# Loading the memory of a cross-attention in four transfers, one feature in eight to a partition

## The chip, the cores and the metric

One core of a Trainium2 chip runs the whole kernel. Its engines work side by side and meet at semaphores: TensorE (PE in the profile; PEld is its weight load), VectorE (DVE), ScalarE (ACT), GpSimd (POOL) and SyncE (SP), which here only starts transfers. ACT and POOL start some transfers too. The metric is the device time of one execution in microseconds; lower is better. Where several executions were timed, the median is used.

## The reference

Two layers of a hybrid network over 256 tokens of 1024 features, batch 1, all in float32. Each layer has four sublayers with a layer norm behind each:

```
for l in range(2):
    h = layer_norm(ALPHA * h + 0.5 * swiglu(h, ffn1_gate[l], ffn1_up[l], ffn1_down[l]))
    z = h @ w_in[l]                      # conv, recurrence and pool from slices of z
    h = layer_norm(ALPHA * h + mix @ w_out[l])
    h = layer_norm(ALPHA * h + cross_attn(h, mem, ca_q[l], ca_k[l], ca_v[l], ca_o[l]))
    h = layer_norm(ALPHA * h + 0.5 * swiglu(h, ffn2_gate[l], ffn2_up[l], ffn2_down[l]))

def cross_attn(x, mem, wq, wk, wv, wo):
    q, k, v = x @ wq, mem @ wk, mem @ wv          # 4 heads of 256
    return softmax(q k^T / 16) v @ wo
```

`mem` is 256 rows of 1024 features. It is an input, the same for both layers, and enters only as `mem @ ca_k[l]` and `mem @ ca_v[l]`: sums over the 1024 features, whose order may be chosen as long as memory and weights use the same one. The feed-forward width is 2816.

## The kernel before

Every float32 product is made of three passes on PE: each operand is split into a rounded part (`hi`, written by ACT as a cast) and the rest (`lo`, written by DVE as a difference), and hi·hi, hi·lo and lo·hi are summed in PSUM. `split` (L74 to L76) makes both parts, so "L75 ACT" and "L76 DVE" in the profile are the parts of weights (`whi`, `wlo`) and of activations. All matmuls are issued from `product` (L126).

Weights come through `load` (L78): DMAs on SP's queue into `raw` buffers (six of 128x1024), then splits into `whi` and `wlo` (eight each). A buffer is used again as soon as its last reader is through, so SP's transfers, the casts on ACT and the differences on DVE each wait for those that released the buffer. Each queue works strictly in its own order. That order comes from a scheduler with its own estimates of time, except in stretches under `manual_schedule`.

A feed-forward net (`ffn`, L420) runs over its 2816 hidden columns in chunks of 512. Chunks 2 and 4 go by `by_seven` (L594), a scheme that needs seven half-products in the place of eight: it adds blocks of weights to each other before multiplying. The blocks are `w00`, `w01`, `w10`, `w11`. Three sums are made on DVE (L624), and two in the transfer itself: `more(w01, up, 1)` and `more(w00, gate, 1)` load a further block on POOL's queue with `accum_op=add` onto what lies there (L658, two transfers of 512 KB each). The second pair can start once DVE has split the earlier contents of `w00`. Its order on PE: `run(o[0], ..., w00)`, `run(o[1], bx[0], ...)`, `run(o[2], ...)`, a slab of the down projection, `run(o[0], bx[1], ...)`, another slab, `run(o[0], bx[2], ...)`, `run(o[3], bx[3], ...)`, `run(o[0], part_of_x(1, 1), parts_of(w00), True)`. Twice between these, `taken` (L653) lets ACT copy the running sum out of `o[0]` before PE adds to it again: `taken(e, o[0])` ahead of the run with `bx[2]`, and `taken(f, o[0])` ahead of the last run, which uses the `w00` of the accumulating transfer. `w00` of chunk 4 lies in the buffers `lng` and `lnb`, into which SP later loads the layer norm's parameters (L316, L317).

The memory is fetched once, during the first feed-forward net. In `load_memory` (L204), called at chunk 3 (L766), 32 transfers on POOL's queue (L213) put feature kP+p into partition p: for each of 8 groups of 128 features and 4 quarters of 32 partitions, 256 runs of 128 bytes (32 features of one row). A small copy ahead of them (L765) holds them until chunk 2's activations exist. They land as 32x32 blocks lying side by side, still turned the wrong way. At chunk 5, `later` (L218) has DVE transpose each block (L222, four instructions of 128x512, reading adjacent elements) and split the result into `mT`. Between L222 and the layer norm behind the net (`finish`, L323), DVE has the last splits of weights, the sums L352 and the norm itself (L362 to L378); PE then transposes the normed rows (L193), first of the first 128 tokens.

`keys` (L789) and `values` (L799) load `ca_k` and `ca_v` by `load` and multiply them with `mT`.

Of the kernel before, what the change touches and what calls it, by code (L numbers as in the profile page):

```python
# [17 lines left out]
P = 128  # L18
DEPTH = 2
SEQ = 256  # L20
DM = 1024
DFF = 2816
NT = SEQ // P
NK = DM // P
# [4 lines left out]
CHUNK = 512  # L29
# [31 lines left out]
def model(ctx: ExitStack, tc: tile.TileContext, t: dict, out: bass.AP):  # L61
    nc = tc.nc
# [5 lines left out]
    def acc(shape=(P, 2, SEQ), tag="acc"):  # L68
        return ps.tile(list(shape), F32, tag=tag, name=tag)


    loads, normed, lows = [], [], []

    def split(hi, lo, src):  # L74
        nc.scalar.copy(hi, src)  # L75
        lows.append(nc.vector.tensor_tensor(lo, src, hi.bitcast(F32), op=ALU.subtract))  # L76

    def load(src, k0, nk, c0, ncol, fine=False, dealt=False):  # L78


        hi, lo, todo = [], [], []
        step = 2048 // ncol
        for a in range(k0, k0 + nk, step):
            half = step // 2
            raw = [
                wp.tile([P, 1024], F32, tag="raw", name="raw", bufs=6).rearrange("p (k c) -> p k c", c=ncol)
                for _ in range(2)
            ]
            part = 1 if fine else half
            for b in range(0, step, part):  # L90
                to = raw[b // half][:, b % half : b % half + part, :]
                if dealt:

                    c, u = divmod(a // 2, 2)
                    at = slice(c * CHUNK + 2 * P * b, c * CHUNK + 2 * P * (b + 1))
                    rows = src[at, c0 : c0 + ncol].rearrange("(p u) c -> p u c", u=2)[:, u, :]
                    loads.append(nc.sync.dma_start(to[:, 0, :], rows))
                else:
                    loads.append(nc.sync.dma_start(
                        to, src[(a + b) * P : (a + b + part) * P, c0 : c0 + ncol].rearrange("(k p) c -> p k c", p=P)  # L100
                    ))
            for s in range(2):
                h = wp.tile([P, 1024], F32R, tag="whi", name="whi", bufs=8)
                w = wp.tile([P, 1024], F32R, tag="wlo", name="wlo", bufs=8)
                h = h.rearrange("p (k c) -> p k c", c=ncol)
                w = w.rearrange("p (k c) -> p k c", c=ncol)
                r = raw[s]
                if fine:
                    todo += [(h[:, b, :], w[:, b, :], r[:, b, :]) for b in range(half)]
                else:  # L110
                    split(h, w, r)
                hi.append(h)
                lo.append(w)
        return Weights(hi, lo, half, todo)
# [3 lines left out]
    def halves(a):  # L118
        return a.rearrange(
            "p (h c) -> p h c" if len(a.shape) == 2 else "p r (h c) -> p r h c", h=2  # L120
        )
# [7 lines left out]
    def sums(o):  # L129
        return o.rearrange("p (c h) -> p h c" if len(o.shape) == 2 else "p r (c h) -> p r h c", h=2)  # L130
# [4 lines left out]
    def mm_cols(w, cols, x):  # L135
        o = acc()
        for k in range(NK - 1):
            product(o, w.at(k, cols)[0], x[:, k], k == 0, False)
        for k in range(NK):
            product(o[:, 0, :], w.at(k, cols)[1], x[:, k, 0, :], False, False)  # L140
        product(o, w.at(NK - 1, cols)[0], x[:, NK - 1], False, True)
        return sums(o)

    def add(dst, o):
        dst = dst if len(dst.shape) == 3 else halves(dst)
        nc.scalar.copy(dst, o[:, 1])
        nc.vector.tensor_tensor(dst, o[:, 0], dst, op=ALU.add)


    def mm_rows(o, xh, xl, wh, wl, start, stop, more=False):  # L150
        product(o, xh, wh, start, False, more)
        product(o, xh, wl, False, False, more)
        product(o, xl, wh, False, stop, more)

    def tok(i):
        return slice(i * P, (i + 1) * P)
# [29 lines left out]
    early_rows, early_memory = (cst.tile([P, 2048], F32, tag=f"mT{n}", name=f"early{n}") for n in range(2))  # L186
# [15 lines left out]


    def load_memory(mp, behind):  # L204
        m = [
            early_memory[:, n * DM : (n + 1) * DM].rearrange("p (k b j) -> p k b j", k=4, j=32) for n in range(2)
        ]
        with tc.issue_after(behind.ins):
            for n in range(2):
                for a in range(4):  # L210
                    for k in range(4):
                        c = (4 * n + k) * P + a * 32
                        nc.gpsimd.dma_start(  # L213
                            m[n][a * 32 : a * 32 + 32, k],
                            t["mem"][0, :, c : c + 32].rearrange("(b i) j -> i b j", i=32),
                        )

        def later():  # L218
            for n in range(2):
                turned = mp.tile([P, NT, CHUNK], F32, tag="up", name="turned", bufs=1)  # L220
                for k in range(2):
                    nc.vector.transpose(turned[:, k, :], m[n][:, 2 * k : 2 * k + 2].rearrange("p k b j -> p (k b j)"))  # L222
                mT.tiles[n] = cst.tile([P, 4, 2, SEQ], F32R, tag=f"mT{n}", name=f"mT{n}")
                for k in range(2):
                    d = slice(4 * n + 2 * k, 4 * n + 2 * k + 2)
                    split(mT[:, d, 0, :], mT[:, d, 1, :], turned[:, k, :].rearrange("p (k t) -> p k t", k=2))

        return later
# [191 lines left out]
    def ffn(l, name, n, pend=None, last=False, early=None):  # L420
        gate, up, down = (t[f"{name}_{x}"][l] for x in ("gate", "up", "down"))
        with tc.tile_pool(name="ffn", bufs=2, reuse_waits="tile") as fp:
# [56 lines left out]
            def first():  # L479

                s = activations()
                wg = load(gate, 0, NK, 0, CHUNK, fine=pend is None)
                wu = load(up, 0, NK, 0, CHUNK) if pend is not None else None

                if pend is None:
# [8 lines left out]
                    with tc.manual_schedule(engines={E.Activation, E.DVE, E.PE}):  # L494
# [43 lines left out]
                        for k in range(2, NK):  # L538
                            if k + 2 < NK:
                                split(*wg.todo[k + 2])  # L540
                            if k < 6:
                                nc.scalar.copy(*whole[k - 2])
                            group(k, 0, 1)
                    wu = load(up, 0, NK, 0, CHUNK)
                    bx.extend(blocks_of_x())
                    ou = all_products(wu)
# [240 lines left out]


    def keys(l, c, between={}):  # L789
        w = load(t["ca_k"][l], 0, NK, c * CHUNK, CHUNK)  # L790
        for p in range(2):
            o = sm.tile([P, 2, SEQ], F32, tag="sums", name="sums", bufs=1)
            for j in range(2):
                between.get(4 * p + 2 * j, lambda: None)()
                add(o[:, j, :], mm_cols(w, slice((2 * p + j) * P, (2 * p + j + 1) * P), mT))
            d = slice(4 * c + 2 * p, 4 * c + 2 * p + 2)
            split(kTh[:, d, :], kTl[:, d, :], o)

    def values(l, c, vh, vl, between={}):  # L799
        w = load(t["ca_v"][l], 0, NK, c * CHUNK, CHUNK)  # L800
        for i in range(NT):
            o = acc((P, 512))
            for k in range(NK):
                if k % 2 == 0:
                    between.get(4 * i + k // 2, lambda: None)()
                wh, wl = w.at(k, slice(0, CHUNK))
                mm_rows(o, mT[:, k, 0, tok(i)], mT[:, k, 1, tok(i)], wh, wl, k == 0, k == NK - 1)
            d = slice(c * CHUNK, (c + 1) * CHUNK)
            split(halves(vh[:, i, d]), halves(vl[:, i, d]), sums(o))
# [343 lines left out]
    def attention(l, pend):  # L1153
        scale = (DM // HEADS) ** -0.5
        with tc.tile_pool(name="att", bufs=1, reuse_waits="tile") as ap:
# [70 lines left out]
            def mixed(hh, pT):  # L1226
# [13 lines left out]

            pT = []
            values(l, 0, vh, vl, {6: pend})
            query(0)
            gb = ln_params(l, 2)
            query(1, lambda: (weights(0), deal(0), weights(1), deal(1)))
            values(
                l, 1, vh, vl,
                {
# [22 lines left out]
    for l in range(DEPTH):  # L1271
        pend = ffn(l, "ffn1", 0, pend, early=None if l else beginnings)
        keys(l, 0, {6: pend})
        pend = mixer(l, lambda: keys(l, 1))
        pend = attention(l, pend)
        pend = ffn(l, "ffn2", 3, pend, last=l == DEPTH - 1)
# [27 lines left out]
```

## Time and profile before

| | us |
|---|---|
| median of 3 runs | 1073.73 (1072.25 to 1074.01) |
| the profiled execution | 1071.91 |
| its span in the trace | 1070.2 |
| PE busy | 1056.5 |
| DVE busy | 913.3 |
| ACT busy | 658.7 |
| POOL busy | 103.4 |
| the 32 transfers of the memory, from issue to landing (median) | 4.5 |

The page gives busy time by engine, the span in 40 slices, the DMA queues, and a chain of waits followed back from the last instruction. The timeline lists instructions in order of time with, in brackets, the idle time of the engine just before and what ended it. A row that ends in x4 merges four like instructions; its duration is that of all of them. DMA rows under POOL or SPq are the issue of a transfer, not the transfer.

### The profile page before, as it was taken

How to read it: one execution, taken by the hardware profiler on the slowest of the kernel's cores; microseconds unless marked ns; L12 is line 12 of the kernel's file. 1: busy time of each engine (PE TensorE's matmuls, PEld its weight loads, DVE VectorE, ACT ScalarE, POOL GpSimd, SP SyncE). 2: the span in 40 equal slices, each digit the busy share in tenths (PEclk: the TensorE clock that was granted, in tenths of full speed). 3: DMA queues.
4: the chain of work that ended last, by engine and by line, in shares of the span. 5: the costliest groups of instructions: out<-in, count | busy, mean ns of one | idle time of the engine just before them, and what ended most of it. 6: DMA issues, size and time to landing. Idle time of an engine off the chain costs nothing.

```text
span 1070.2 us, 16349 instructions
## 1 busy us (share of the span) xinstructions
PE 1056.5 (99%) x5954; PEld 936.2 (87%) x5954; DVE 913.3 (85%) x1225; ACT 658.7 (62%) x903; POOL 103.4 (10%) x147
## 2 busy tenths in 40 slices
PE   9999989999999999999999999999999999999997
PEld 7888878989889888888888888888898998888886
DVE  6998688989998798897698988789899788889876
ACT  7675575768466556656475757566774665665661
POOL 8003501000000001010001000010000000000000
PEclk9999999999999999999999999999999999999999
DMA  9998984754574589979578988857636665799861
GB/s 364 292 312 266 226 295 135 259 198 141 194 262 169 184 269 240 358 187 298 179 268 233 333 227 255 261 180 229 196 111 232 236 231 177 237 293 300 222 208 40
DMA packets 139601, 248.70 MB, mean 232 GB/s; under 512 B 9920, under 2 KB 49120, under 8 KB 139520
## 3 DMA queue, kind: packets, MB, share of 16 engines
q1 hardware_dynamic: 129024, 228.49, 63.9%
q0 software_dynamic: 9920, 17.98, 9.8%
q10 hardware_dynamic: 576, 1.18, 0.3%
q8 instruction: 47, 0.77, 0.3%
q14 instruction: 34, 0.28, 0.1%
HBM read 232.93 MB, written 1.05 MB: 219 GB/s over the span
## 4 chain that ended last, share of the span: by engine, by line
PE 93%; DMA 3%; DVE 2%; issue 1%; POOL 1%; ACT 1%; DVEq 0%; ACTq 0%; POOLq 0%
PE acc L126 63%; PE dn L126 27%; PE acc L193 1%; DMA early<-in_mem_dram 1%; DMA raw<-in_ffn_gate_dram 1%; POOL early L213 1%; DMA h<-in_x_dram 1%; PE dn L989 0%; ACT whi L75 0%; PE dn L1063 0%; DVE wlo L76 0%; DVE turned L222 0%; DVE h L378 0%; DVE mT L76 0%; PE dn L1062 0%
## 5 line engine op out<-in xcount | busy, mean ns | idle before, releaser
L76 DVE TENSOR_TENSOR wlo<-raw,whi 128x1024 fp32r<-128x1024 f32 (+1 forms) x444 | 525.0, 1210 | 64.9 <-ACT whi L75 50.6
L75 ACT CAST whi<-raw 128x1024 fp32r<-128x1024 f32 (+1 forms) x444 | 449.2, 1042 | 203.9 <-PE acc L126 63.0
L126 PE MATMUL acc<-whi,xT 128*128 128x512 f32 x992 | 302.0, 381 | 3.2 <-ACT halves L653 3.2
L126 PEld LDWEIGHTS acc<-whi,xT 128*128 128x128 f32 x992 | 188.4, 190 | 30.4 <-ACT halves L653 3.6
L126 PE MATMUL acc<-wlo,xT 128*128 128x512 f32 x496 | 188.7, 381 | 0.0
L126 PE MATMUL acc<-xT,whi 128*128 128x512 f32 x576 | 141.0, 381 | 0.2
L126 PE MATMUL dn<-whi,ah 128*128 128x512 f32 x346 | 131.5, 380 | 0.0
L126 PE MATMUL dn<-wlo,ah 128*128 128x512 f32 x346 | 131.1, 379 | 0.0
L126 PE MATMUL dn<-whi,al 128*128 128x512 f32 x346 | 131.1, 379 | 0.0
L126 PEld LDWEIGHTS acc<-xT,whi 128*128 128x128 f32 x576 | 104.1, 190 | 12.5 <-ACT whi L75 0.8
L126 PEld LDWEIGHTS acc<-wlo,xT 128*128 128x128 f32 x496 | 94.0, 190 | 13.3
L126 PE MATMUL dn<-whi,xT 128*128 128x512 f32 x288 | 87.8, 381 | 0.0
L126 PEld LDWEIGHTS acc<-xT,wlo 128*128 128x128 f32 x576 | 75.5, 191 | 3.8
L126 PE MATMUL acc<-xT,wlo 128*128 128x256 f32 x576 | 75.9, 275 | 0.0
L126 PEld LDWEIGHTS dn<-whi,al 128*128 128x128 f32 x346 | 65.4, 189 | 9.3
L126 PEld LDWEIGHTS dn<-wlo,ah 128*128 128x128 f32 x346 | 65.4, 189 | 9.2
L126 PEld LDWEIGHTS dn<-whi,ah 128*128 128x128 f32 x346 | 65.4, 189 | 9.1
L126 PEld LDWEIGHTS dn<-whi,xT 128*128 128x128 f32 x288 | 54.4, 189 | 7.6 <-DVE xT L76 0.2
L370 POOL TENSOR_TENSOR rs<-rs,nhalf 128x1 f32<-128x1 f32 x16 | 15.0, 935 | 451.8 <-DVE rs L366 320.8
L126 PE MATMUL dn<-wlo,xT 128*128 128x512 f32 x144 | 54.6, 379 | 0.0
L126 PE MATMUL acc<-whi,kTh 128*128 128x512 f32 x128 | 48.5, 379 | 0.0
L126 PE MATMUL acc<-wlo,kTh 128*128 128x512 f32 x128 | 48.5, 379 | 0.0
(240 smaller groups left out, 1297.3 us busy)
## 6 DMA issues: line engine op xcount, KB each, us to landing
raw<-in_ffn_up_dram SPq DMA_DIRECT2D x88, 512.0 KB, 5.9
raw<-in_ffn_down_dram SPq DMA_DIRECT2D x88, 512.0 KB, 5.9
raw<-in_ffn_gate_dram SPq DMA_DIRECT2D x84, 512.0 KB, 5.5
raw<-in_w_in_dram SPq DMA_DIRECT2D x48, 512.0 KB, 4.5
dealt<-sg SPq DMA_DIRECT2D x80, 128.0 KB, 4.9
raw<-in_ffn_up_dram POOLq DMA_DIRECT2D x16, 512.0 KB, 6.1
raw<-in_ffn_gate_dram POOLq DMA_DIRECT2D x16, 512.0 KB, 9.8
raw<-in_ca_k_dram SPq DMA_DIRECT2D x16, 512.0 KB, 5.6
```

The source lines that it names most:

```text
L75: nc.scalar.copy(hi, src)
L76: lows.append(nc.vector.tensor_tensor(lo, src, hi.bitcast(F32), op=ALU.subtract))
L126: nc.tensor.matmul(o, w, x, start=start, stop=stop, skip_group_check=more)
L193: nc.tensor.transpose(pt[:, k, :], src[:, (4 * j + k) * P : (4 * j + k + 1) * P], unit)
L213: nc.gpsimd.dma_start(m[n][a * 32 : a * 32 + 32, k], t["mem"][0, :, c : c + 32].rearrange("(b i) j -> i b j", i=32),)
L370: nc.gpsimd.tensor_tensor(rs, rs, nhalf[:, 0:1], op=ALU.pow)
```

## The change

The memory is laid out the other way: feature 8p+k lies in partition p. Then the 32 partitions of a quarter hold 256 adjacent features, and one transfer for each quarter moves 256 runs of 1 KB. Within a partition the elements of one k are 8 apart (32 bytes), so the transposes read with that step. `ca_k` and `ca_v` are loaded with their rows in the same order (`across`): partition p receives rows 8p+k, for each load two k, which are adjacent rows.

```diff
-    def load(src, k0, nk, c0, ncol, fine=False, dealt=False):
+    def load(src, k0, nk, c0, ncol, fine=False, dealt=False, across=False):
...
+                elif across:
+                    rows = src[:, c0 : c0 + ncol].rearrange("(p k) c -> p k c", p=P)
+                    loads.append(nc.sync.dma_start(to, rows[:, a + b : a + b + part, :]))
...
     def load_memory(mp, behind):
-        m = [
-            early_memory[:, n * DM : (n + 1) * DM].rearrange("p (k b j) -> p k b j", k=4, j=32) for n in range(2)
-        ]
+        m = early_memory.rearrange("p (b j k) -> p k b j", b=8, k=NK)
         with tc.issue_after(behind.ins):
-            for n in range(2):
-                for a in range(4):
-                    for k in range(4):
-                        c = (4 * n + k) * P + a * 32
-                        nc.gpsimd.dma_start(
-                            m[n][a * 32 : a * 32 + 32, k],
-                            t["mem"][0, :, c : c + 32].rearrange("(b i) j -> i b j", i=32),
-                        )
+            for a in range(4):
+                nc.gpsimd.dma_start(
+                    early_memory[a * 32 : a * 32 + 32].rearrange("p (b f) -> p b f", b=8),
+                    t["mem"][0, :, a * 256 : (a + 1) * 256].rearrange("(b i) f -> i b f", i=32),
+                )
...
-                    nc.vector.transpose(turned[:, k, :], m[n][:, 2 * k : 2 * k + 2].rearrange("p k b j -> p (k b j)"))
+                    nc.vector.transpose(
+                        turned[:, k, :].rearrange("p (k b j) -> p k b j", k=2, j=32),
+                        m[:, 4 * n + 2 * k : 4 * n + 2 * k + 2],
+                    )
...
-        w = load(t["ca_k"][l], 0, NK, c * CHUNK, CHUNK)
+        w = load(t["ca_k"][l], 0, NK, c * CHUNK, CHUNK, across=True)
...
-        w = load(t["ca_v"][l], 0, NK, c * CHUNK, CHUNK)
+        w = load(t["ca_v"][l], 0, NK, c * CHUNK, CHUNK, across=True)
```

PE's order of instructions is the same in both programs. ACT's and DVE's differ in a few neighbouring places in chunk 4 of the first net (the cast of the first `w00` buffer stands ahead of the first L653, its difference two places earlier), and one load of `w_down` on SP stands ahead of four small transfers in the place of behind them.

## Prediction

> **What bounds the kernel now.** First the page: TensorE (PE) is busy almost all of the span, so a change can gain only where PE stands still or runs slowly.
>
> ```profile
> span 1070.2 us, 16349 instructions
> PE 1056.5 (99%) x5954; PEld 936.2 (87%) x5954; DVE 913.3 (85%) x1225; ACT 658.7 (62%) x903; POOL 103.4 (10%) x147
> ```
>
> Then the busy time by stage, to find the 13.7 us in which PE is not busy (columns: stretch, its length, busy time and count of PE, of its weight loads, DVE, ACT, POOL, granted PE clock, DMA share, GB/s).
>
> ```profile
> 0.00:40.00 40.00, 37.70 (x173) 32.17 (x174) 30.04 (x36) 26.77 (x37) 23.95 (x52) 1.00 0.93 332
> 134.00:138.20 4.20, 1.04 (x5) 0.59 (x5) 3.52 (x4) 4.20 (x6) 0.00 (x0) 1.00 0.64 217
> 157.00:177.00 20.00, 19.76 (x94) 17.03 (x92) 17.39 (x28) 10.86 (x16) 1.92 (x2) 1.00 0.48 163
> 200.00:1000.00 800.00, 799.90 (x4698) 711.53 (x4697) 693.13 (x953) 498.09 (x707) 43.32 (x45) 1.00 0.73 229
> 1060.00:1070.20 10.20, 2.42 (x22) 2.23 (x20) 5.32 (x13) 0.00 (x0) 0.92 (x1) 0.83 0.21 78
> ```
>
> Start (2.3 us) and end (7.8 us) belong to any run. Between 200 and 1000 us PE loses 0.1 us. One hole is left, 3.2 us at 134.9 to 138.0, and a nick of 0.24 us before 177. The timeline of PE shows the hole and what it costs behind it.
>
> ```profile
> 134.27 0.38 PE L126 MATMUL acc<-wlo,kTh 128*128 128x512 f32 x1
> 134.48 0.38 PE L126 MATMUL acc<-whi,kTl 128*128 128x512 f32 x1
> 138.02 0.58 PE L126 MATMUL acc<-whi,xT 128*128 128x512 f32 x1 [3.15 <-ACT halves L653]
> ```
> ```profile
> 138.02:142.18 4.16, 4.16 (x11) 0.59 0.73 259
> ```
>
> Matmuls start 0.215 us apart (134.27 to 134.48). The next should start at 134.70 and starts at 138.02: 3.32 us lost. Then 11 matmuls take 4.16 us instead of 11 x 0.216 = 2.37, at a granted clock of 0.59: 1.79 us more. **The hole costs 5.1 us in all.**
>
> Who makes it: PE waits for ACT's copy of `o[0]` (`taken(f, o[0])`, L653), and ACT, which works in order, stands in front of it for the accumulating loads of `w00` (L658).
>
> ```profile
> 124.59 0.59 ACT L653 COPY halves<-acc 128x512 f32<-128x512 f32 x1 [0.94 <-PE acc L126]
> 130.87 1.04 ACT L75 CAST whi<-raw 128x1024 fp32r<-128x1024 f32 x1 [5.69 <-DMA raw<-in_ffn_gate_dram]
> 133.60 3.88 ACT L75 CAST whi<-raw 128x1024 fp32r<-128x1024 f32 x4 [1.69 <-DMA raw<-in_ffn_gate_dram]
> 137.39 0.57 ACT L653 COPY halves<-acc 128x512 f32<-128x512 f32 x1
> ```
>
> Those two loads stand on POOL's queue behind the 32 transfers of the memory:
>
> ```profile
> 100.60 4.69 POOL L213 DMA_DIRECT2D early<-in_mem_dram  x8 [0.30 <-POOL early L765]
> 106.06 7.53 POOL L213 DMA_DIRECT2D early<-in_mem_dram  x13 [0.77 <-DMA early<-in_mem_dram]
> ...
> 121.96 2.55 POOL L658 DMA_DIRECT2D raw<-in_ffn_gate_dram  x2 [0.35 <-issue]
> ```
>
> **Part 1: 32 transfers become 4.** One issue takes 4.69/8 = 0.59 us on POOL. Four take 2.3 us: from 100.60 POOL is through at 102.9, not 121.6. Each still has 256 rows (32 partitions by 8), so I keep the price of one; were it that of L658 (2.55/2 = 1.28 us), POOL would be through at 105.7, which changes nothing below. What then holds the two L658 is their own data: DVE must have split `w00` (after `w11` was added to it), which by the order of instructions are the third and fourth of this group:
>
> ```profile
> 108.84 5.11 DVE L76 TENSOR_TENSOR wlo<-raw,whi 128x1024 fp32r<-128x1024 f32 x4 [1.72 <-ACT whi L75]
> ```
>
> That is 108.84 + 3 x 1.28 = 112.7 and 114.0. The L658 are issued at these times, 9.2 us earlier than at 121.96 and 123.2. From issue to landing they took 8.9 us (121.96 to 130.87) and 10.4 (123.2 to 133.60). The same stage of the next FFN, with no memory in front of it, gives the worst case, and shows PE without a hole:
>
> ```profile
> 477.07 2.43 POOL L658 DMA_DIRECT2D raw<-in_ffn_gate_dram  x2 [14.15 <-DVE wlo L76]
> ```
> ```profile
> 488.66 1.05 ACT L75 CAST whi<-raw 128x1024 fp32r<-128x1024 f32 x1 [0.23 <-DMA raw<-in_ffn_gate_dram]
> ```
> ```profile
> 461.00:512.00 51.00, 51.00 (x254) 1.00 0.90 251
> ```
>
> 477.07 to 488.66 is 11.6 us, so the new landings are at 124.3 and 125.6 at the latest. The build moves one instruction here: the cast of the first `w00` now stands before the first L653 (`taken(e, o[0])`), not behind it. So L653 runs at 124.3 + 1.05 = 125.4 instead of 124.59. PE needs it at 129.52, when `run(o[0], bx[2], ...)` continues in that bank: 3.6 us to spare. (Two runs of 12 matmuls end at 134.70; 24 x 0.216 before it is 129.52, 12 x 0.216 is 132.11.) The second L653 can then follow PE at some 132.4, and is needed at 134.70. Hole and slow clock go: **-5.1 us**. SP's queue is freed as well (its load of `lng`, L316, waited for the same `w00`), so the `w_down` rows behind it come earlier.
>
> **Part 2: the turn with a stride.** The four transposes (L222) read elements 32 bytes apart instead of adjacent ones. They lie here (DVE, then PE):
>
> ```profile
> 162.67 1.62 DVE L76 TENSOR_TENSOR al<-sg,ah 128x256 fp32r<-128x256 f32 x2 [1.00 <-ACT ah L75]
> 164.22 1.29 DVE L222 STREAM_TRANSPOSE turned<-early 128x512 f32<-128x512 f32 x2
> 165.44 1.17 DVE L76 TENSOR_TENSOR wlo<-raw,whi 128x1024 fp32r<-128x1024 f32 x1
> ...
> 168.87 1.29 DVE L222 STREAM_TRANSPOSE turned<-early 128x512 f32<-128x512 f32 x2
> ...
> 175.69 1.41 DVE L378 SCALAR_TENSOR_TENSOR h<-h,rs,lnb 128x512 f32<-128x512 f32 x2
> ```
> ```profile
> 175.97 0.38 PE L126 MATMUL dn<-whi,al 128*128 128x512 f32 x1
> ```
>
> DVE works from 162.67 without a gap into the layer norm, whose first half (L378, done at 176.4) PE needs for L193. PE's last matmul before it starts at 175.97, so L193 was due at 176.19 and starts at 176.59: DVE is already 0.4 us late. **Nothing hides the transposes: each extra microsecond is one of PE's.** DVE's run starts from buffers that PE releases, so it moves ahead with PE by the same 5.1 us and brings no slack.
>
> No row shows a transpose that reads at 32 bytes. Nearest are L1142, which writes at 16 bytes, and L958, whose step is 8 bytes in the first row below and which has longer runs in the second:
>
> ```profile
> 265.72 1.54 DVE L1142 STREAM_TRANSPOSE yr<-dealt 128x512 f32<-128x512 f32 x1
> 267.04 0.59 DVE L888 TENSOR_SCALAR sg<-sg,prm 128x256 f32<-128x256 f32 x2
> ```
> ```profile
> 268.74 1.13 DVE L1142 STREAM_TRANSPOSE yr<-dealt 128x512 f32<-128x512 f32 x1
> 269.70 0.42 DVE L147 TENSOR_TENSOR sums<-acc,sums 128x256 f32<-128x256 f32 x1
> ```
> ```profile
> 219.06 0.79 DVE L958 TENSOR_TENSOR k<-k,f 128x512 f32<-128x512 f32 x1 [0.61 <-PE dn L1014]
> ```
> ```profile
> 224.16 0.68 DVE L958 TENSOR_TENSOR k<-k,tot 128x512 f32<-128x512 f32 x1
> ```
>
> From start to the next start, a contiguous transpose takes (165.44 - 164.22)/2 = 0.61 us, L1142 1.32 and 0.96: 0.35 to 0.71 more, mean 0.53. The 8-byte step costs 0.11 more. Below: nothing makes a stride faster, so 0.0 to 0.11. Above: if the price doubles again from 16 to 32 bytes, 2 x 0.71 = 1.4. I take 0.53, the nearest row: 4 x 0.53 = **+2.1 us**, between 0 and 5.7.
>
> [...]
>
> **Part 3: `across` for `ca_k` and `ca_v`.** Rows 8p+k in the place of kP+p: still 2 KB runs, 256 per load, the same bytes and the same SP issues. Only the addresses differ. The loads are early. The first `ca_k` is issued from 150.41 and its matmuls stand behind the L193 of 176.59; of `ca_v`, the second cast comes right upon landing, and the third and fourth wait 9.6 us for PE.
>
> ```profile
> 150.41 6.76 SPq L99 DMA_DIRECT2D raw<-in_ca_k_dram  x4
> ```
> ```profile
> 280.79 1.05 ACT L75 CAST whi<-raw 128x1024 fp32r<-128x1024 f32 x1 [0.93 <-DMA raw<-in_ca_v_dram]
> 291.43 1.99 ACT L75 CAST whi<-raw 128x1024 fp32r<-128x1024 f32 x2 [9.60 <-PE dn L126]
> ```
>
> So a few us of slower landing are hidden, by 19 us of PE work behind the last `ca_k` issue (157.2 to 176.6) and by those 9.6 us: 0. Without that cover each late us would be one of PE's.
>
> **Sum:** -5.1 + 2.1 = -3.0 us. The profiled execution had 1070.2 us of span; 3.0 less is 1067.2. The median of the runs shown is 1073.73 (1072.25 to 1074.01); against it the forecast is **1070.7 us**.
>
> **Rivals.**
>
> 1. *The stride is free.* For: an 8-byte step costs only 0.11. Against: L1142. Then only the hole goes: 1073.7 - 5.1 = 1068.6.
>
> 2. *A second slow clock.* With +2.1, PE waits 0.4 + 2.1 = 2.5 us at L193. A wait of 3.15 us halved the clock; whether 2.5 does, no row shows. If so, 1.8 comes back: 1073.7 - 3.0 + 1.8 = 1072.5, within what counts as no change. [...] Here 3.15 us sufficed, so the measurement leaves the case open.
>
> 3. *Slower: the transposes cost more than the hole.* Place: L222 ahead of the layer norm; price: 1.4 each, 5.7 in all, and the wait at L193 of 6.1 us halves the clock again (1.8): -5.1 + 5.7 + 1.8 = +2.4, 1076.1. It decides from 4x + 1.8 > 5.1, x = 0.83 us each. For: the price rose steeply from 8 to 16 bytes. Against: the dearest row has 0.71, below that point.
>
> 4. *It doesn't do what it says.* The accumulating loads land late all the same; with the cast now ahead of the first L653, PE would stop at 129.5 instead. That needs a landing over 15 us after 112.7; the worst seen is 11.6. The time stays: 1073.7 + 2.1 = 1075.8 at worst.
>
> **How the numbers follow.** Forecast 0.47, rival 1 0.18, rival 2 with its neighbours (price 0.7 to 0.9) 0.17, rival 3 0.12, rival 4 0.06. 0.2% (2.15 us) is about what a measurement can tell from no change. Forecast (a gain of 2.3 to 3.7) and rival 1 are faster, less a few in the margin: 0.63. Rival 2 and that margin: 0.20. Rivals 3 and 4: 0.17. The range goes from rival 1 less the spread of the runs (0.8) to 1074.5, which leaves out rival 3 and half of rival 4. The forecast's own range is 1069.3 to 1072.2.
>
> **What will show it.** (By the line numbers of before.) Right: four L213 issues on POOL and L658 at about 113; no wait of PE for L653 and a granted clock of 1.00 from 134 to 142; L222 at 1.1 to 1.4 us; PE waiting 2 to 3 us for L378 before L193 at about 171 to 174, the only new hole. Wrong: L222 at 0.65 as now (then 1068.6) or above 1.5 us (no gain); a clock near 0.5 behind L193; a PE wait near 129.5; or waits of ACT for `ca_k` or `ca_v` that PE feels.

## The result, and the profile after

| | before | after |
|---|---|---|
| median, first set (6 runs each) | 1073.75 | 1068.54 (1068.29 to 1070.62) |
| median, second set (26 and 10 runs) | 1073.02 | 1070.07 (1068.42 to 1070.80) |
| profiled execution | 1071.91 | 1068.35 |
| its span | 1070.2 | 1066.6 |

The ratio of after to before is 0.9960 (95%: 0.9947 to 0.9973) in the first set and 0.9974 (0.9965 to 0.9983) in the second: faster by 5.2 and by 2.95 us. The profiled executions differ by 3.6 us. Why three numbers come out, and not one, is part of what the experiments show. Line numbers after the change are one to three higher, except L222 (now L220) and L213 (now L211).

First the stages of the changed kernel, in the columns of the table by stage that the prediction opens with:

```profile
134.00:138.20 4.20, 4.20 (x21) 3.69 (x20) 4.20 (x5) 3.83 (x4) 0.00 (x0) 1.00 0.78 265
138.20:157.00 18.80, 18.80 (x105) 16.90 (x104) 14.70 (x17) 11.15 (x16) 0.00 (x0) 1.00 0.90 296
157.00:177.00 20.00, 18.03 (x87) 15.44 (x86) 18.06 (x27) 11.67 (x17) 1.92 (x2) 1.00 0.29 87
```

The stretch from 134.0 to 138.2, in which PE had been busy for 1.04 us, is full, and behind it the clock is 1.00. A new hole of 2 us stands between 157 and 177, where there was one of 0.24. The timelines of POOL and of ACT show the first part of the change:

```profile
100.53 2.41 POOL L211 DMA_DIRECT2D early<-in_mem_dram  x4 [0.30 <-POOL early L766]
112.88 2.51 POOL L659 DMA_DIRECT2D raw<-in_ffn_gate_dram  x2 [9.94 <-DVE wlo L76]
```
```profile
121.61 2.92 ACT L75 CAST whi<-raw 128x1024 fp32r<-128x1024 f32 x3
124.52 0.59 ACT L654 COPY halves<-acc 128x512 f32<-128x512 f32 x1
...
132.24 0.59 ACT L654 COPY halves<-acc 128x512 f32<-128x512 f32 x1 [0.24 <-PE acc L129]
```

Four issues take 2.41 us, POOL then stands idle until DVE has split `w00`, and the accumulating loads go out at 112.88 and not at 121.96. No cast in this stretch waits for a DMA any more, and the second copy of `o[0]` starts at 132.24 and not at 137.39. The timelines of DVE and PE show the second part:

```profile
159.05 2.15 DVE L220 STREAM_TRANSPOSE turned<-early 128x512 f32<-128x512 f32 x2
161.06 1.24 DVE L76 TENSOR_TENSOR wlo<-raw,whi 128x1024 fp32r<-128x1024 f32 x1
...
164.49 2.18 DVE L220 STREAM_TRANSPOSE turned<-early 128x512 f32<-128x512 f32 x2
166.51 0.73 DVE L353 SCALAR_TENSOR_TENSOR h<-h,dn 128x512 f32<-128x512 f32 x1
```
```profile
170.79 0.38 PE L129 MATMUL dn<-whi,al 128*128 128x512 f32 x1
173.10 1.29 PE L196 MATMUL acc<-idn,h 128*128 128x128 f32 x8 [1.93 <-DVE h L379]
```

From start to next start a pair takes 2.01 us where it took 1.22: 0.40 us more for each transpose. PE pays it: it waits 1.93 us ahead of the layer norm's matmuls.

### The profile page after: what moved, and what is told of

The parts are those of the page before. It is cut to its first block, busy times and chain, and to the rows that moved or that the text cites. A ratio compares the mean times of both kernels' runs of the same rounds, so it can differ in the third digit from the quotient of the medians.

```text
span 1066.6 us, 16319 instructions
## 1 busy us (share of the span) xinstructions
PE 1054.6 (99%) x5954; PEld 935.1 (88%) x5954; DVE 915.1 (86%) x1225; ACT 658.8 (62%) x903; POOL 87.2 (8%) x119
## 3 DMA queue, kind: packets, MB, share of 16 engines
HBM read 232.93 MB, written 1.05 MB: 219 GB/s over the span
## 4 chain that ended last, share of the span: by engine, by line
PE 97%; DVE 2%; DMA 0%; issue 0%; ACT 0%; DVEq 0%; ACTq 0%
PE acc L129 65%; PE dn L129 29%; PE acc L196 1%; DMA h<-in_x_dram 0%; PE dn L990 0%; DVE turned L220 0%; DVE wlo L76 0%; PE dn L1064 0%; DVE mT L76 0%; DVE h L379 0%; PE dn L1063 0%; PE dn L1052 0%; PE acc L1132 0%; DVE h L374 0%; PE dn L1015 0%
```

## The experiments

They are told by question, not in the order in which they ran.

### Which part does what

`e3_across_alone` is before with only the new order of the rows of `ca_k` and `ca_v`; the memory stays in the old order.

```diff
-        w = load(t["ca_k"][l], 0, NK, c * CHUNK, CHUNK)
+        w = load(t["ca_k"][l], 0, NK, c * CHUNK, CHUNK, across=True)
...
-        w = load(t["ca_v"][l], 0, NK, c * CHUNK, CHUNK)
+        w = load(t["ca_v"][l], 0, NK, c * CHUNK, CHUNK, across=True)
```

> The kernel before, with only the rows of ca_k and ca_v loaded in the new order, so that keys and values are products with features in the wrong order. Theory: nothing on PE's path, span 1070.2 plus or minus 0.3, ratio 1.000. Rival (addresses 32 KB apart load slower or faster and PE feels it): casts wait for ca_k or ca_v longer than 0.9 us and the span moves by 1 us or more.

Measured: 1073.02 us against 1072.45, ratio 1.0000 (0.9988 to 1.0012). PE's waits in it:

```profile
PE acc L129 <- ACT halves L656: 3.8, 1, 3.8
PE acc L196 <- DVE h L381: 0.3, 1, 0.3
```

The hole is there as before, and the order of the rows costs nothing that can be measured.

`e4_two_features` changes the layout to feature 256g+2p+k: 16 transfers with rows of 256 bytes, and transposes that read 8 bytes apart. The order on ACT around `taken` stays that of before. The main line of the edit, against the changed kernel (the transfers and the rows of the weights follow it):

```diff
-        m = early_memory.rearrange("p (b j k) -> p k b j", b=8, k=NK)
+        m = early_memory.rearrange("p (g b j k) -> p g k b j", g=4, b=8, k=2)
...
```

> Between the two kernels: feature 256g+2p+k in partition p, 16 transfers with runs of 256 bytes, transposes that read 8 bytes apart; weight rows to match. Theory: 16 issues of 0.59 us end at about 111, ahead of the 112.7 at which w00 is ready, so no hole; a step of 8 bytes costs 0.1 us or less for each transpose, so PE waits 0.3 to 0.7 us before L193; span 1065.1 to 1065.6, ratio 0.9955. Rival (any stride costs the same 0.4 us): wait of 1.9 us, span 1066.6. Rival (the hole went because a cast was moved ahead of L653, which here stays in its old order): a hole of some 3 us, span 1069 to 1070.

Measured: 1068.16 us (1067.60 to 1069.32), ratio 0.9953 (0.9939 to 0.9968). Transposes take 0.76 us, PE waits 0.85 us ahead of the layer norm, and there is no hole at 134. The gain is there with 16 issues as with 4, without the moved cast. The span of 1066.4 is above what was expected. Part of that is the start, of which more below: PE's first net begins at 8.25 us in this execution and at 7.44 in after's.

`e1_behind` keeps the layout of before and moves the 32 transfers behind the accumulating loads, which are collected in `added`.

```diff
...
-                    nc.gpsimd.tensor_copy(early_memory[:, 0:2048:256], acts[2][0][:, 0, 0:8].bitcast(F32))
-                    turn_memory = load_memory(fp, loads[-1])
+                if c == 4 and early is not None:
+                    with tc.issue_after(added[-1].ins):
+                        nc.gpsimd.tensor_copy(early_memory[:, 0:2048:256], acts[2][0][:, 0, 0:8].bitcast(F32))
+                    turn_memory = load_memory(fp, added[-1])
```

> The kernel before with its 32 transfers of the memory and its contiguous transposes; only the place on POOL's queue changes: the 32 transfers stand behind the accumulating loads of w00 instead of ahead of them. Theory (POOL's queue makes the hole, the stride costs 0.4 us for each transpose on PE's path): the two L658 are issued at about 113, no hole at L653, granted clock 1.00 from 134 to 142, transposes at 0.65 us, PE waits 0.2 to 0.4 us at L193; span 1065.1 against 1070.2 before and 1066.6 after, ratio to before 0.995. Rival (the 8192 small packets of 128 bytes crowd the DMA engines and make the accumulating loads late, wherever they stand): a hole of 1 to 3 us remains or moves to the loads of w_down behind it; span 1067 to 1070.

Measured: 1070.58 us (1067.77 to 1071.60, 12 runs), ratio 0.9976 (0.9965 to 0.9986), span 1068.2. The hole is gone, but the time is 3 us above what I expected. Its trace shows where, first in the issues of the memory on POOL, then in DVE's and PE's timelines:

```profile
116.73 3.54 POOL L213 DMA_DIRECT2D early<-in_mem_dram  x6 [0.30 <-POOL early L767]
...
142.94 1.16 POOL L213 DMA_DIRECT2D early<-in_mem_dram  x2 [0.31 <-DMA early<-in_mem_dram]
```
```profile
152.15 1.30 DVE L471 STREAM_TRANSPOSE square<-dealt 128x512 f32<-128x512 f32 x2 [3.46 <-DMA dealt<-sg]
```
```profile
174.65 1.29 PE L193 MATMUL acc<-idn,h 128*128 128x128 f32 x8 [2.70 <-DVE h L378]
```

The small transfers are now issued until 144 us, beside the four that turn the fifth chunk's product (`dealt`, `turn`, L466). DVE waits 3.46 us for these, which take 8.1 us from issue to landing where they took 6.3 in the changed kernel, and is late for the layer norm without any stride. That the small transfers make them slow is likely and not shown: they took 7.2 us in `e5` below, where no small transfer ran beside them. So the price that I had put on the stride is a price on anything that makes DVE late there.

`e2_stride_alone` was meant to be after's layout loaded by 32 transfers in their old place.

> The changed kernel's layout, stride and row order, but the memory again in 32 transfers of 128-byte runs. Theory: the hole of 3.3 us and the slow clock of 1.8 us are back, and the four transposes take 1.0 us each instead of 0.65, so that PE also waits 1.9 us before L193; span 1070.2 + 1.6 = 1071.8, ratio 1.0015. Rival (the stride is hidden as long as the hole gives DVE time to get ahead): span 1070.2, PE waits 0.2 us before L193. Rival (8 rows apart in ca_k and ca_v is what moved the time): span about 1066.6.

```diff
-            for a in range(4):
+            for s in range(8):
+                for a in range(4):
...
```

It did not test that. The small copy covered only four of the 32 slices, and the other 28 were issued between 22 and 44 us, away from the hole. Measured: 1069.26 us, ratio 0.9963 (0.9949 to 0.9977), no hole, PE waiting 1.95 us ahead of the layer norm. Its six runs lie in two groups, 1068.3 (three) and 1070.1 to 1070.3 (three). `e7_stride_held` mends it: the copy covers all 32 slices.

```diff
-    nc.gpsimd.tensor_copy(early_memory[:, 0:2048:256], acts[2][0][:, 0, 0:8].bitcast(F32))
+    nc.gpsimd.tensor_copy(early_memory[:, 0:2048:32], acts[2][0][:, 0, 0:64].bitcast(F32))
```

> The changed kernel's layout and strided turn, but loaded by 32 transfers, all of them held back to the place that they have before the change. By my sum: the hole of 3.3 us and the slow clock behind it (1.8) are back, and the strided transposes cost 4 x 0.4 = 1.6 us more, though the hole lets DVE's work run on: PE waits about 1.9 us ahead of the layer norm; span 1070.2 + 1.6 = 1071.8. Rival (the stride is hidden as long as the hole is there): span 1070.2, with a wait below 0.5 us ahead of the layer norm.

Measured: 1075.44 us against 1073.02, ratio 1.0019 (1.0008 to 1.0030); spans 1071.6 to 1075.1. The issue of its accumulating loads, its waits of PE and two stages:

```profile
122.93 2.46 POOL L660 DMA_DIRECT2D raw<-in_ffn_gate_dram  x2 [0.65 <-DVE s L304]
```
```profile
PE acc L196 <- DVE h L380: 4.1, 1, 4.1
PE acc L129 <- ACT halves L655: 3.3, 1, 3.3
```
```profile
138.20:157.00 18.80, 18.42 (x101) 16.60 (x102) 15.24 (x18) 12.31 (x15) 0.00 (x0) 1.00 0.97 307
...
177.00:200.00 23.00, 20.68 (x111) 18.73 (x112) 19.81 (x32) 14.82 (x22) 3.14 (x5) 0.85 0.52 162
```

With the 32 issues back, the accumulating loads go out at 122.93 and the hole is back. The stride alone makes the kernel slower, by 2.4 us in the medians and by 2.6 between the lowest spans of the set (1071.6 against before's 1069.0), where 1.6 had been expected. What the rest is stays open: the profiled execution has the highest span, and in it DVE also waited 2.46 us for `dealt`, and the clock was halved behind the wait of 4.1 us ahead of the layer norm (0.50 from 179 to 183, 0.85 over the stretch from 177 to 200). The rival (a stride hidden by the hole) falls.

### What the stride costs

`e11_four_features` lies between the two: feature 512n+4p+k, 8 transfers, a step of 16 bytes. The main line of the edit, with the transfers and the rows of the weights to match:

```diff
-        m = early_memory.rearrange("p (b j k) -> p k b j", b=8, k=NK)
+        m = early_memory.rearrange("p (g b j k) -> p g k b j", g=2, b=8, k=4)
...
```

> Feature 512n+4p+k in partition p: 8 transfers with rows of 512 B, and transposes that read 16 bytes apart. A contiguous one took 0.61 us from start to next start, at 8 bytes 0.75, at 32 bytes 1.01. If the price follows the step, 16 bytes give 0.85 to 0.90 us, PE waits 1.3 to 1.5 us ahead of the layer norm, span 1066.0 to 1066.3, and the clock falls in few runs. [...]

Measured: 1072.12 us against 1072.41, ratio 0.9997 (0.9988 to 1.0006). The expectation doesn't hold; the step of 16 bytes is dearer than that of 32 (1.44 against 1.01 us). From DVE's timeline:

```profile
159.43 2.94 DVE L223 STREAM_TRANSPOSE turned<-early 128x512 f32<-128x512 f32 x2
162.30 1.18 DVE L76 TENSOR_TENSOR wlo<-raw,whi 128x1024 fp32r<-128x1024 f32 x1
```

That is 1.44 us each. PE waits 3.57 us ahead of the layer norm, and the change gains nothing. `e12_steps` asks whether the step itself does this.

```diff
+                if n == 0:
+                    to = [turned[:, k, :].rearrange("p (k b j) -> p k b j", k=2, j=32) for k in range(2)]
+                    steps = lambda s: early_memory[:, 0 : 256 * s].rearrange("p (b j k) -> p k b j", b=8, k=s)[:, 0:2]
+                    nc.vector.transpose(to[0], steps(2))
+                    nc.vector.transpose(to[1], steps(2))
...
+                    nc.vector.transpose(to[1], steps(8))
```

> A measurement of the disputed price by itself: the changed kernel with 14 more transposes of 128x512 ahead of its own four, two each with reads 8, 12, 16, 20, 24, 28 and 32 bytes apart, all from the loaded memory; their results are overwritten. The time of the whole is of no interest (DVE is about 14 us later, PE waits that much). If the step alone sets the price: 0.76 us from start to next start at 8 bytes, 1.44 at 16 and 1.01 at 32, as in the three layouts. If the price grows with the bytes spanned: 8 < 12 < 16 < 20 < 24 < 28 < 32, and 16 bytes at 0.85 to 0.9, so that the 1.44 belongs to something else in that kernel (DMA writing at the same time, the place in memory). If only powers of two are dear: 12, 20 and 28 bytes at or below 0.8.

Measured (one run of 1080.84 us, in which PE waits 11.6 us). DVE's timeline, two lines of code for each step from 8 bytes (L222, L223) to 32 (L234, L235):

```profile
159.41 0.86 DVE L222 STREAM_TRANSPOSE turned<-early 128x512 f32<-128x512 f32 x1
...
160.93 1.15 DVE L224 STREAM_TRANSPOSE turned<-early 128x512 f32<-128x512 f32 x1
...
163.09 1.50 DVE L226 STREAM_TRANSPOSE turned<-early 128x512 f32<-128x512 f32 x1
...
165.92 1.12 DVE L228 STREAM_TRANSPOSE turned<-early 128x512 f32<-128x512 f32 x1
...
168.02 1.08 DVE L230 STREAM_TRANSPOSE turned<-early 128x512 f32<-128x512 f32 x1
...
172.04 1.09 DVE L234 STREAM_TRANSPOSE turned<-early 128x512 f32<-128x512 f32 x1
...
174.05 2.03 DVE L237 STREAM_TRANSPOSE turned<-early 128x512 f32<-128x512 f32 x2
```

Half the distance between these starts is the time of one: 0.76 us at 8 bytes, 1.08 at 12, 1.42 at 16, 1.05 at 20, and 1.0 at 24 to 32, against 0.61 for adjacent elements. The three steps that the layouts use cost here what they cost there (0.76, 1.44 and 1.01 us), so the step sets the price, and the price does not grow steadily with the bytes. A step of 8 bytes is cheaper than any longer one, but dearer than adjacent elements (0.76 against 0.61 us), and one of 16 is dearer than one of 32 (1.42 against 1.0). Why, no run shows.

### Where the price falls, and how it is avoided

`e8_turn_twice` does the second pair of strided transposes twice.

```diff
-                    nc.vector.transpose(
+                    for _ in range(1 + n):
+                        nc.vector.transpose(
...
```

> The changed kernel with the second pair of transposes done twice: two more of 1.0 us each in front of the layer norm. By my reading every microsecond there is one of PE's, so PE waits 1.9 + 2.0 = 3.9 us, and a wait so long lowers the clock in nearly every run (1.8 us more): 1068.4 + 2.0 + 1.8 = 1072.2, in one group. Rival (the clock's fall does not hang on the length of this wait): two groups still, about 1070.4 and 1072.2. Rival (something hides the transposes): 1068.4.

Measured: 1072.01 us (1071.60 to 1073.29, 10 runs in one group), ratio 0.9992 (0.9983 to 1.0002). PE and the clock behind its wait:

```profile
175.08 1.71 PE L196 MATMUL acc<-idn,h 128*128 128x128 f32 x8 [3.92 <-DVE h L380]
```
```profile
177.00:179.00 2.00, 2.00 (x6) 1.63 (x5) 2.00 (x4) 1.31 (x2) 0.00 (x0) 0.50 0.27 33
```

Two more transposes, 2.0 us on DVE, are 2.0 us more of waiting for PE (3.92 against 1.93), and the clock is halved behind it. Nothing hides the turn in its place.

`e9_after_turned_sooner` is the changed kernel with the turn one chunk sooner.

```diff
-                if c == 5 and early is not None:
+                if c == 4 and early is not None:
```

> The changed kernel with the turn of the memory put one chunk sooner: the four strided transposes and the splits behind them stand on DVE ahead of the transposes of the fifth chunk's product instead of ahead of the layer norm. If the whole price of the stride is that DVE is late for the layer norm, and DVE has room in the stage from 138 to 157 us (4.1 us idle there in the changed kernel), the wait of PE ahead of the layer norm falls below 0.5 us: span 1066.6 - 1.9 = 1064.7, with runs in one group. Rival (the stage has no room: the turn and its splits take 7 to 8 us of DVE, more than the 4.1 us): the turned product of the fifth chunk is late, PE waits as long there or at the layer norm, span 1066.6 or more.

Measured: 1066.77 us (1066.29 to 1067.27, 4 runs), ratio 0.9945 (0.9932 to 0.9959), span 1064.6. The strided transposes cost what they did, but DVE has room for them there. Its timeline, and the stages:

```profile
141.33 2.15 DVE L220 STREAM_TRANSPOSE turned<-early 128x512 f32<-128x512 f32 x2
143.36 1.23 DVE L76 TENSOR_TENSOR wlo<-raw,whi 128x1024 fp32r<-128x1024 f32 x1
...
166.34 0.69 DVE L353 SCALAR_TENSOR_TENSOR h<-h,dn 128x512 f32<-128x512 f32 x1 [2.41 <-PE dn L129]
```
```profile
138.20:157.00 18.80, 18.80 (x104) 16.89 (x104) 18.55 (x22) 12.58 (x19) 0.00 (x0) 1.00 0.82 257
157.00:177.00 20.00, 19.89 (x100) 17.19 (x99) 15.30 (x27) 11.04 (x15) 2.15 (x4) 1.00 0.48 155
```

DVE's 4.1 idle us from 138 to 157 are used up (18.55 of 18.80), and now it waits 2.41 us for PE ahead of the layer norm, not the other way round.

`e5_contiguous_early` takes the other way out: the layout of before, without the copy that holds the transfers back.

```diff
-                    nc.gpsimd.tensor_copy(early_memory[:, 0:2048:256], acts[2][0][:, 0, 0:8].bitcast(F32))
```

> The layout, the 32 transfers and the contiguous turn of before, but without the small copy that holds the transfers back, so that POOL issues them in the first 40 us. If the gain of the change is only that the accumulating loads no longer queue behind 32 issues, and the stride is pure loss: no hole near 134, transposes at 0.61 us each, PE waiting about 0.3 us ahead of the layer norm's matmuls, span 1065.0 (1070.2 less 5.1), 1.6 below the changed kernel's 1066.6, and runs that lie close together because no wait is long enough to lower the clock. Rival: the many small rows crowd the start, where DMA is 0.93 busy and PE waits for its first weights: then PE idles longer in the first 40 us (more than 2.3 us) and the span is 1067 or above.

Measured: 1067.47 us (1066.62 to 1068.16), ratio 0.9949 (0.9936 to 0.9962); spans 1064.9 to 1066.5. No hole; the 32 small transfers, issued between 21 and 47 us, cost PE nothing that shows (38.05 us busy in the first 40, 37.80 after the change, and all of the time from 20 to 50). Of the profiled execution, the slowest of the six, 1.07 us is a wait ahead of the layer norm that I had not expected: DVE waits 1.13 us for `dealt` there. Why that lands later in it than in after's (7.2 against 6.3 us from issue to landing, in the median) stays open. `e10_early_turned_sooner` puts the turn one chunk sooner here too.

> The contiguous layout loaded in the first 40 us, with the turn one chunk sooner. It had waited 1.1 us ahead of the layer norm. If DVE has room in the stage from 138 to 157 us that wait goes: span 1064.5 to 1065.5, about 1 us below the same kernel with the turn in its old place. Rival (no room): the fifth chunk's product comes later, span 1066.5 or more.

Measured: 1066.64 us (1066.42 to 1066.67, 5 runs), ratio 0.9943 (0.9930 to 0.9957), span 1064.9. It and e9 are the fastest, and can't be told apart: once the hole is gone and the turn has room, the layout decides nothing that could be measured.

### Why the runs spread

`e6_after_again` is the changed kernel once more.

> The changed kernel once more, beside the others of this set. PE waits 1.9 us ahead of the layer norm's matmuls in every run; if that wait sometimes lowers the clock and sometimes not, the runs fall into two groups, about 1068.4 and 1070.4 us, some 1.8 us apart. If the two groups come from elsewhere, the kernel without that wait shows them too.

Measured: 1070.07 us. Of all 16 runs of this kernel, 7 lie at 1068.3 to 1068.6 and 9 at 1069.7 to 1070.8. The first profile fell in the lower group (span 1066.6), this one in the upper (1069.1). PE's wait ahead of the layer norm is the same, but what follows isn't. First two rows of this execution, then one of the first:

```profile
174.16 1.29 PE L196 MATMUL acc<-idn,h 128*128 128x128 f32 x8 [1.87 <-DVE h L379]
```
```profile
176.00:178.00 2.00, 2.00 (x6) 1.55 (x6) 2.00 (x3) 1.51 (x3) 0.00 (x0) 0.50 0.32 23
```
```profile
175.00:177.00 2.00, 2.00 (x11) 1.76 (x10) 2.00 (x3) 1.94 (x4) 0.00 (x0) 1.00 0.26 39
```

At half the clock PE does 6 matmuls in 2 us where it did 11. From L196 of the first 128 tokens to that of the second it takes 13.3 us (174.16 to 187.43) in place of 11.6 (173.10 to 184.68): 1.7 us. Another 1.2 us are the kernel's start, where PE begins slow in both traces (the first five matmuls of 128x512, from 1.52 on, take 2.50 us, so they start 0.43 apart and not 0.22), but not equally long. PE's timelines of the first profile and of this one:

```profile
5.24 0.48 PE L493 MATMUL dn<-kTh 128*128 128x512 f32 x1
...
7.44 0.68 PE L129 MATMUL dn<-whi,xT 128*128 128x512 f32 x2
```
```profile
5.35 0.78 PE L493 MATMUL dn<-kTh 128*128 128x512 f32 x1
...
8.65 0.68 PE L129 MATMUL dn<-whi,xT 128*128 128x512 f32 x2
```

Together that is 2.9 us, and the spans differ by 2.5. The length of the wait goes with the spread: kernels without it (e9, e10) have all their runs within 1.0 us, at 0.85 and 1.07 us (e4, e5) the runs lie within 1.8, at 1.9 (after, e2) in two groups, and at 3.92 (e8) all lie in one, behind a slow clock in the trace. But length alone does not decide: the profiled execution of e1 waits 2.70 us and keeps a clock of 1.00. The last section shows what else does.

## Why the prediction was right, and where it was not

**The hole and the slow clock (-5.1): right.** The accumulating loads went out at 112.88 (112.7 predicted), the copies of `o[0]` ran at 124.52 and 132.24 (125.4 at the latest, and 132.4), PE is busy from 134.0 to 138.2, and the clock is 1.00 behind. Of the 5.1, the 1.8 of the slow clock belong to the profiled execution: the same hole in e7 left the clock at 1.00. E3 and e7 have the 32 issues in the old place and the hole; after, e2, e4, e5 and e11 don't, and have none.

**The turn (+2.1): right in place, too dear.** It cost 4 x 0.40 = 1.6 us, and e8 shows that PE pays for each microsecond (1.99 us more of waiting for 2.0). The step of the working that was off is the choice of the nearest row. L1142 writes 16 bytes apart, and among reads 16 is the dearest step of all (1.42 us in e12): nearest in the number was not nearest in the cost. What a write costs by its step no run shows. With 1.6 the sum is -3.5, and the two spans differ by 3.6.

**`across` (0): right.** E3 shows it.

**Rival 2, the second slow clock, given 0.17: it happens, in some runs.** A wait of 1.87 us halved the clock in e6, and one of 1.93 in after did not (last section), and 9 of 16 runs lie in the upper group, though the start's part isn't separated in those without a profile. The forecast treated it as a thing that either is or isn't. That also bears on the medians. The sum was made on a profiled execution (1071.91) that lay 1.8 us below the median of its three runs; its -3.0 stands against -3.6 from profile to profile, while the median moved by 5.2 or 2.95, with how many runs of the changed kernel fell into which group. Before's own runs spread over 4.5 us, and what parts them is not shown, as only one of them has a trace. How near 1070.7 comes to a median (0.6 us off the second, 2.2 off the first) hangs on that mixture and says little about the sum. The 1068.5 of the first set would have been taken for rival 1 (a free stride, 1068.6) by anyone who looked at the time alone; the trace shows the stride paid.

**Rival 3, transposes dearer than the hole: not here, but at 16 bytes.** There one costs 1.44 - 0.61 = 0.83 us more, which was the point from which it decides, and e11 comes out at the time of before. **Rival 4** (late landings) falls: no cast waits for them.

The cause that the change is worth something is thus not the layout but that no issues hold up POOL's queue any more when the two accumulating loads could go out. That was tried in both directions: e4 (16 issues, done in time), e5 and e10 (32 issues, long done) have the gain with other layouts, e7 has the layout with 32 issues in the way and no gain. The moved cast is not needed either: e4 has it in the old place.

## What to carry to other kernels

When an engine stalls on a transfer, look at what stands ahead of that transfer on its queue: here 32 issues of 0.6 us delayed two loads that had nothing to do with them, and issuing the 32 earlier (e5) was worth at least as much as making them 4. Before paying for a strided read to get longer rows, put the turn where its engine has idle time; in the same place it was 1.6 us on the critical path, one chunk sooner nothing. Price a step with the same step and direction, not with the nearest number, and compare profile with profile, since a median can move with the mixture of its runs.

## What was not expected of the hardware

In e12 a transpose of 128x512 float32 that reads 16 bytes apart takes 1.42 us, at 12 and 20 bytes 1.05 to 1.08, at 24 to 32 bytes 1.0 and at 8 bytes 0.76.

The clock is not tied to the length of a wait alone. In e7 a hole of 3.3 us at 135 left it at 1.00, and so did 2.70 us in e1, while in before 3.15 us at the same place as e7's halved it, and 1.87 us did so in e6. A slow clock in the middle of a trace lasts 3.41 us (before, e2, e3, e6, e8, e11) or a multiple of it (6.83 in e7, 13.65 in e12); in before it is 3.413. What decides shows when the whole time is cut into stretches of that length, counted from the moment at which the clock first stands at 1.00 (8.52 us in e6). In the rows, as in the table by stage, the first number behind the comma is PE's busy time, and the clock stands third from the end. They are of e6, after, before and e7: two waits at the layer norm and two holes.

```profile
172.36:175.78 3.42, 1.58 (x11) 1.35 (x12) 3.42 (x7) 2.24 (x4) 1.68 (x2) 1.00 0.00 0
175.78:179.19 3.41, 3.41 (x10) 2.69 (x9) 2.98 (x4) 2.64 (x4) 0.00 (x0) 0.50 0.47 113
```
```profile
169.08:172.49 3.41, 2.09 (x10) 1.50 (x8) 2.06 (x7) 2.95 (x4) 1.43 (x2) 1.00 0.00 0
172.49:175.90 3.41, 2.76 (x16) 2.40 (x17) 3.41 (x6) 2.17 (x4) 0.49 (x1) 1.00 0.00 0
```
```profile
134.86:138.27 3.41, 0.26 (x2) 0.26 (x2) 3.41 (x4) 3.41 (x5) 0.00 (x0) 1.00 0.60 210
138.27:141.69 3.42, 3.42 (x9) 2.72 (x9) 3.42 (x5) 2.54 (x3) 0.00 (x0) 0.50 0.73 261
```
```profile
133.52:136.93 3.41, 1.73 (x9) 1.17 (x7) 1.69 (x2) 2.76 (x3) 0.00 (x0) 1.00 0.47 155
136.93:140.35 3.42, 1.77 (x8) 1.58 (x9) 3.42 (x4) 3.42 (x6) 0.00 (x0) 1.00 0.66 199
140.35:143.76 3.41, 3.41 (x22) 3.09 (x21) 3.41 (x5) 2.14 (x4) 0.00 (x0) 1.00 0.99 338
```

The waits in e6 (but for 0.03 us) and in before lie in one stretch, and the next one runs at 0.50. Those in after and e7 are shared between two, and the clock stays. In before and after each fall and each recovery of the clock lies on this grid, within 0.01 us: in before the clock stands at 1.00 for 133.12 us from 5.16 on and for 925.01 us behind the slow stretch, which are 39 and 271 stretches of 3.4133, and in after for 1058.13 us from 5.24 on, which are 310. In e6 it recovers at 179.19, 170.67 us behind 8.52, which are fifty. Of the stretches of all traces that ran at 1.00, every one in which PE stood idle for 1.98 us (e2) or more is followed by one at 0.50, and none with 1.78 us (e1) or less is. Between these four stretches, all of e6 and e11, go both ways: 1.84 us halved the clock in both, 1.85 and 1.88 us behind the last matmul of the kernel did not. So the limit lies near 1.8 to 1.9 us in these traces, and idle time as the trace shows it, in which PE's ends are modelled, may not be quite what counts. The grid begins at another time in each of these executions (5.16 us in before, 5.24 in after, 8.52 in e6), so where a wait falls on it differs, and one kernel has both outcomes.

A stretch need not be idle throughout: in e6 1.84 of 3.42 us, little more than half, was enough. No run moved a wait across the grid on purpose.
